# Odd layer's entry: the norm of x ahead of the norm of ctx, both key tiles from one pass over x, values of x between, two query projections in other banks

## The chip, the cores and the metric

The kernel runs on one core of one Trainium2 chip. The metric is the time of one execution on the device in microseconds (us). The time before is the median of three runs, 1648.93 us (1645.26 to 1651.0). TensorE is called PE below, VectorE DVE, ScalarE ACT, GpSimd POOL; SP is the engine whose queue issues nearly all transfers.

## The reference

A block of two layers on a sequence of 512 tokens (x) and 256 context tokens (ctx) of width 1024. The change lies where layer 0 ends (its feed-forward part, for x and ctx) and layer 1, the odd one, begins:

```python
def rmsnorm(x, g):
    xf = x.astype(jnp.float32)
    y = xf * lax.rsqrt(jnp.mean(xf * xf, axis=-1, keepdims=True) + EPS)
    return (y * g.astype(jnp.float32)).astype(x.dtype)

def modulate(x, g, shift, scale):
    return rmsnorm(x, g) * (1 + scale) + shift

def odd_mixer(h, hc, w_qkv, w_out, sink, cos, sin, need_ctx):
    q, k, v = jnp.split(h @ w_qkv, [C_Q_WIDTH, C_Q_WIDTH + C_KV_WIDTH], axis=-1)
    q = apply_rope(q.reshape(b, s_len, C_HEADS, HEAD_DIM), cos, sin)
    k = apply_rope(k.reshape(b, s_len, C_KV_HEADS, HEAD_DIM), cos, sin)
    kc, vc = jnp.split(hc @ w_qkv[:, C_Q_WIDTH:], 2, axis=-1)
```

So x and ctx, both modulated, give keys and values (4 key/value heads of 64, that is two key tiles of 128 rows and one value block of 256 columns); x alone gives queries (16 heads, eight query tiles of 128 rows). Each block of 128 queries attends to a window of up to three blocks of x and to all of ctx, with a sink in the softmax. Output projection, residual and the second feed-forward part follow.

## The kernel before, in words

Activations lie transposed in SBUF: width along the 128 partitions in 8 tiles (k or m, 0 to 7), tokens along the free axis (512 of x, 256 of ctx). All is fp32; a product is made of three matmuls at fp32r (`mm3`, L95, the lines L99, L100, L101): high part by high part, high by low, low by high. So each operand exists as a high part (a cast or copy, by ACT) and a low part (the difference, by DVE or POOL).

Weights come through a ring (`open_ring`, L54; `unit`, L67): SP issues a transfer of 512 columns into a `raw` buffer, ACT casts it to the high part (L75), POOL subtracts for the low part (L78), both into a `w` slot. In `odd` the ring has three raw buffers and four slots (`self.open_ring(512, 3, 4)`). A slot or raw buffer is taken again when its last reader is done; a pool opened in the room of one that closed waits for the last readers of what lay there.

PSUM has three pools of accumulators: `bank` (L45, three buffers, named pb), `fill` (L48, one buffer, pf), and `wide` (L51, two buffers of two banks, pw). Buffers of a pool are given out in turn, in the order in which the program asks for them.

A scheduler puts the instructions of each engine into one fixed list; each engine works through its list in order and stands still at an instruction whose inputs or buffers are not ready. `issue_after(ins)` holds what stands in its block until behind that instruction in the lists.

The stretch that the change touches, in the order of the program:

1. End of the first feed-forward part (L1070 to L1120): for x and then for ctx, the last eight products, each followed by the residual (L757, DVE) and the square (`square`, L769, ACT). The squares of the eight tiles are partly added up (L773, DVE or POOL; tiles 0 to 3) and partly left apart (the list `rest`; tiles 4 to 7).
2. `modulated` for x, then for ctx. Each begins with `rstd_rows` (L135): PE sums squares down the partitions with matmuls against ones (L149 for the sum, L153 for the rest), DVE reads one column per block of 128 tokens (L156) and makes the reciprocal root with integer and Newton steps (L128 to L132; 4 columns for x, 2 for ctx), writes diagonal blocks (L165), and PE spreads them with another product against ones (`spread`, L175). The eight tiles are then modulated (`modulate`, L188): L191 on DVE gives t, L192 on ACT the high part ax, L193 on DVE the low part.
3. `odd`: transfers of the rope tables, the mask and the sink. Then `project_k(0)` and `project_k(1)`: weights of the key tile, all eight k for x, all eight for ctx into one wide buffer, then rope (`rope`, L240: L243 and L244 on DVE, L245 and L246 on POOL), and `stack_k` (L262): casts by ACT (L268, L269) and differences by DVE (L271) that put high and low parts on either half of the partitions.
4. Values: three banks hold six blocks of 128 tokens (four of x, two of ctx), two to a bank; for each k all six blocks. Copies to SBUF at L1168.
5. For each of four groups g: two query tiles (`project_q`, eight products of 512 columns each into `fill`, so one buffer for all eight; then rope and `stack_q`, L253 to L259), then `attend(g, 0)`. An `attend` has for two blocks of queries: four score products (`softmax`, L1200 to L1208, in a wide buffer), their maximum (L1211, DVE), the exponential (L1214, ACT), transposes (L1237, PE) into banks, copies out of them (L1240), and products with the values (L1248, PE) into a bank. After the four groups come four `attend(g, 1)`, then the output projection. The scheduler mixes query products into the attention before them or after them.

Of the kernel before, what the change touches and what calls it, by code (L numbers as in the profile page):

```python
# [6 lines left out]
F32 = mybir.dt.float32  # L7
F32R = mybir.dt.float32r
# [6 lines left out]
P = 128  # L15
D = 1024
KT = D // P
TX = 512
TC = 256
TA = TX + TC  # L20
# [6 lines left out]
class Builder:  # L27
# [39 lines left out]
    def unit(self, src, cols, t=None):  # L67

        nc = self.nc
        w, rb, _ = self.ring_cfg  # L70
        raw = self.ring.tile([P, w], F32, name=self.uid("raw"), tag="raw", bufs=rb)[:, :cols]
        self.last_w = nc.sync.dma_start(raw, src)
        t = t or self.slot()
        hi, lo = t[:, 0, :cols], t[:, 1, :cols]
        nc.scalar.copy(hi, raw)  # L75
        self.nu += 1
        eng = nc.vector if self.dve_lo and self.nu % self.dve_lo == 0 else nc.gpsimd
        eng.tensor_tensor(lo, raw, hi.bitcast(F32), ALU.subtract)  # L78
        return hi, lo

    def blocks(self, src, cols=1024, step=P, t=None):

        w = min(self.ring_cfg[0], cols)
        out = []
        for c in range(0, cols, w):
            n = min(w, cols - c)
            hi, lo = self.unit(src[:, c:c + n], n, t)
            out += [(hi[:, i:i + step], lo[:, i:i + step]) for i in range(0, n, step)]
        return out

# [41 lines left out]
            ve.scalar_tensor_tensor(y, t, 1.5, y, ALU.add, ALU.mult)  # L132
        return y

    def rstd_rows(self, acc, T, inv, bank=None, dg=None, more=(), out=None):  # L135
        return self.spread(self.rstd_diag([(acc, T)], inv, bank, None, dg, more)[0], out or bank)

    def rstd_diag(self, accs, inv, bank=None, eps=None, at=None, more=()):

        nc = self.nc  # L140
        nb = sum(T for _, T in accs) // P
        ms = self.small(nb)
        o = 0
        for acc, T in accs:
            ps = (bank or self.bank)()
            n = T // P
            for j in range(n):
                c = slice(j * P, (j + 1) * P)
                nc.tensor.matmul(ps[:, c], acc[:, c], self.ones, start=j == 0, stop=not more, skip_group_check=True)  # L149
            for t in more:  # L150
                for j in range(n):
                    c = slice(j * P, (j + 1) * P)
                    nc.tensor.matmul(ps[:, c], t[:, c], self.ones, start=False, stop=t is more[-1], skip_group_check=True)  # L153
            col = ps[:, 0:T].rearrange("p (j f) -> p j f", f=P)[:, :, 0]
            if eps is None:
                nc.vector.tensor_scalar(ms[:, o:o + n], col, inv, EPS, ALU.mult, ALU.add)  # L156
# [5 lines left out]
        for acc, T in accs:  # L162
            dg = at if at is not None else self.tmp()
            for j in range(T // P):
                self.last_diag = nc.vector.tensor_scalar(dg[:, j * P:(j + 1) * P], self.ident, r[:, o + j:o + j + 1], None,  # L165
                                                         ALU.mult)
            dgs.append(dg[:, :T])
            o += T // P
        return dgs

    def spread(self, dg, bank=None):

        T = dg.shape[-1]
        out = (bank or self.bank)()
        self.nc.tensor.matmul(out[:, :T], self.ones, dg, start=True, stop=True)  # L175
        return out[:, :T]

    def squares(self, hs, T):
# [593 lines left out]
        elif m:  # L772
            (eng or self.nc.vector).tensor_tensor(sq[:, off:off + n], sq[:, off:off + n], t, ALU.add)  # L773

    def modulated(self, l, sq, off, n, more):

        r = self.rstd_rows(sq[:, off:off + n], n, 1.0 / D, self.bank if off == TX else self.fill, None, more)
        for k in range(KT):
            for w, c, _ in self.cols(off, n):
                self.modulate(self.h(w, k)[:, c], n, self.modcol(l, 1, k, w), self.modcol(l, 0, k, w), r,  # L780
                              [t[:, off:off + n] for t in self.A[k]])


    def ffn_open(self, l, room=None):
# [55 lines left out]
    def ffn(self, l):  # L840
        tc, nc, a = self.tc, self.nc, self.a
        both = l == 0
        self.close_ring()
        T = self.T
        NH = T // 2
        Tp = tc.alloc_tile_pool(name=f"T{l}", bufs=1, side="left", reuse_waits="tile")
# [27 lines left out]
        q = [(m0[:, :NH], m0[:, NH:], m1[:, :NH], m1[:, NH:]) for m0, m1 in zip(self.M[:4], self.M[4:])]  # L874
# [19 lines left out]
        raws, sums, state, Wd, gates = {}, {}, {}, {}, {}  # L894
# [198 lines left out]
        q0 = (4, 5)[l]  # L1093
        more, sqs = [], []
# [25 lines left out]

    def odd(self):
        tc, nc, a = self.tc, self.nc, self.a
        self.open_ring(512, 3, 4)
        X, C = [[[t[:, c] for t in A] for A in self.A] for c in (slice(0, TX), slice(TX, TA))]
        self.hcp.release()
        Rk = tc.alloc_tile_pool(name="kv1", bufs=1, side="right", reuse_waits="tile")
        Rt = tc.alloc_tile_pool(name="rope1", bufs=1, side="right", reuse_waits="tile")
        self.ropep = Rk
        tabs = [self.load(Rk, a[n], [P, TX], n) for n in ("cos", "sin")]
        mraw = self.load(Rt, a["mask"], [P, 384], "mraw")  # L1130
# [9 lines left out]
        K = []  # L1140

        def project_k(n):
            W = self.blocks(a["k1"][n])
            kf = Rt.tile([P, TA], F32, name=self.uid("kf"), tag="kf", bufs=1)
            ps = self.wide()
            for off, T, A in ((0, TX, X), (TX, TC, C)):
                self.dense(ps[:, off:off + T], W, A)
            self.rope(ps[:, :TX], kf[:, :TX], tabs)
            nc.scalar.copy(kf[:, TX:], ps[:, TX:TA])
            K.extend(self.stack_k(kf, Rk, TA, "k1", 8))  # L1150

        for n in range(2):
            project_k(n)

        V = []
        bk = [self.bank() for _ in range(3)]
        acc = [b[:, h * TC:(h + 1) * TC] for b in bk for h in range(2)]
        for kq in range(2):
            W = self.blocks(a["v1"][kq], step=256)
            for i in range(4):  # L1160
                k = kq * 4 + i
                for tb in range(6):
                    A = [X[k][p][:, tb * P:(tb + 1) * P] if tb < 4 else C[k][p][:, (tb - 4) * P:(tb - 3) * P]
                         for p in range(2)]
                    self.mm3(acc[tb], A, W[i], k == 0 and tb % 2 == 0, k == KT - 1)
        for tb in range(6):
            v = Rk.tile([P, TC], F32, name=f"v1_{tb}")
            (nc.vector.tensor_copy if tb % 2 else nc.scalar.copy)(v, acc[tb])  # L1168
            V.append(v)
# [93 lines left out]
        raw = {}  # L1263
# [16 lines left out]
        sq = self.sumsq()  # L1280
# [114 lines left out]
```

## Time and profile before

| what | us |
| --- | --- |
| median of three runs | 1648.93 |
| profiled execution | 1649.09 |
| its span in the trace | 1647.3 |
| mean granted clock of PE | 0.976 |
| PE busy in the span | 1541.4 |
| last ctx product of layer 0 begins | 966.22 |
| spread of x's norm begins | 970.14 |
| first key product begins | 972.84 |
| query tile 0 begins | 1013.55 |
| query tile 1 begins | 1021.79 |
| query tile 5 begins | 1056.07 |

The table's starts are on the trace's own clock, from the start of the span. In the lines of a time view the first number is the start, the second the time from the first start to the last end of the instructions grouped in the row (x4 is four of them); then engine, line of the kernel, operation, output and input by the program's names, and shapes; in brackets the idle time of the engine just before and the instruction that ended it. In a table by stretches the columns are the stretch, its length, busy time and count of PE, PE's weight load, DVE, ACT and POOL, then the granted clock of PE as a share of full speed, the busy share of the DMA engines, and GB/s. With PE alone only its column is there.

### The profile page before, as it was taken

Reading aid. Unit: us, or ns where it says so; the run is one execution under the profiler, and the core shown is the slowest. Engines: PE = TensorE matmul, PEld = TensorE weight load, DVE = VectorE, ACT = ScalarE, POOL = GpSimd, SP = SyncE. Lnnn points to the kernel's source line nnn. Section 1 sums busy time; section 2 is a strip of 40 time slices with the busy share of each in tenths; the row PEclk is TensorE's granted clock in tenths of the full one; section 3 lists DMA queues with packets and bytes.
Section 4 is the critical chain, followed back from the end, with each engine's and each line's share of the span. In section 5 each row is a group of like instructions: output and inputs, shape, how many; then the busy total and the mean of one; then the engine's idle time right before and its main releaser. Section 6 shows DMA issues by size and latency. Waiting matters only on the chain.

```text
span 1647.3 us, 24642 instructions
## 1 busy us (share of the span) xinstructions
PE 1541.4 (94%) x9547; PEld 1366.6 (83%) x9547; DVE 1081.8 (66%) x1991; ACT 719.9 (44%) x1460; POOL 766.9 (47%) x543
## 2 busy tenths in 40 slices
PE   6999989989989999999999999999988999999996
PEld 4776878889988889989989878777868989898886
DVE  4622788866766787666666485666667857666665
ACT  2423675634543233333333244556664544444443
POOL 0463121051166667666666415531313466675662
PEclk9999989989999899999999989999999999999998
DMA  8844100122122333443432012100224132323201
GB/s 316 298 171 149 39 7 1 65 82 112 63 103 94 112 122 125 138 153 115 137 132 90 27 50 79 63 28 19 77 104 141 56 111 90 103 90 103 90 27 52
DMA packets 47957, 161.98 MB, mean 98 GB/s; under 512 B 5472, under 2 KB 9952, under 8 KB 40160
## 3 DMA queue, kind: packets, MB, share of 16 engines
q1 hardware_dynamic: 47696, 160.28, 28.5%
q8 instruction: 75, 1.23, 0.3%
q14 instruction: 42, 0.34, 0.1%
q10 hardware_dynamic: 144, 0.13, 0.1%
HBM read 158.29 MB, written 2.10 MB: 97 GB/s over the span
## 4 chain that ended last, share of the span: by engine, by line
PE 67%; DVE 14%; POOL 5%; DMA 5%; ACT 4%; issue 4%; POOLq 0%; SPq 0%; DVEq 0%; ACTq 0%
PE pw L99 8%; PE pw L100 8%; PE pw L101 8%; PE pb L99 7%; PE pb L100 7%; PE pb L101 7%; POOL w L908 4%; DMA raw<-ffn_in 3%; PE pf L99 2%; PE pf L100 2%; PE pb L1248 2%; PE pf L101 2%; PE pb L1237 2%; DMA rawo<-ffn_out 2%; DVE t L959 2%
## 5 line engine op out<-in xcount | busy, mean ns | idle before, releaser
L99 PE MATMUL pw<-ax,w 128*128 128x384 f32 (+2 forms) x732 | 237.2, 328 | 16.2 <-DVE q L1003 6.6
L78 POOL TENSOR_TENSOR w<-raw,w 128x512 fp32r<-128x512 f32 (+1 forms) x84 | 127.8, 1529 | 248.6 <-ACT w L75 219.5
L100 PE MATMUL pw<-ax,w 128*128 128x384 f32 (+2 forms) x732 | 238.0, 326 | 2.7 <-DVE ax L456 1.3
L101 PE MATMUL pw<-ax,w 128*128 128x384 f32 (+2 forms) x732 | 236.1, 324 | 2.1 <-POOL w L908 2.1
L908 POOL TENSOR_TENSOR w<-raw,w 128x512 fp32r<-128x512 f32 x119 | 179.1, 1519 | 53.0 <-ACT w L904 53.0
L908 POOL TENSOR_TENSOR w<-t,w 128x512 fp32r<-128x512 f32 x90 | 133.6, 1484 | 135.3 <-ACT w L904 131.9
L99 PE MATMUL pb<-hh,w 128*128 128x512 f32 x480 | 167.8, 362 | 13.4 <-ACT hh L115 7.4
L100 PE MATMUL pb<-hh,w 128*128 128x512 f32 x480 | 171.7, 359 | 1.0 <-POOL hh L116 1.0
L101 PE MATMUL pb<-hh,w 128*128 128x512 f32 x480 | 171.2, 358 | 0.0
L757 DVE SCALAR_TENSOR_TENSOR xT<-pb,mod,xT 128x512 f32<-128x512 f32 (+3 forms) x208 | 144.2, 703 | 39.4 <-PE pb L101 38.7
L99 PEld LDWEIGHTS pw<-ax,w 128*128 128x128 f32 x732 | 141.5, 194 | 27.6 <-DVE q L1003 8.2
L99 PE MATMUL pw<-T,w 128*128 128x384 f32 (+1 forms) x508 | 158.7, 313 | 4.9 <-DVE hs L999 2.5
L100 PE MATMUL pw<-T,w 128*128 128x384 f32 (+1 forms) x508 | 158.1, 311 | 4.0 <-DVE T L116 4.0
L101 PE MATMUL pw<-T,w 128*128 128x384 f32 (+1 forms) x508 | 157.6, 310 | 0.0
L100 PEld LDWEIGHTS pw<-ax,w 128*128 128x128 f32 x732 | 142.2, 194 | 11.0 <-DVE ax L456 3.1
L101 PEld LDWEIGHTS pw<-ax,w 128*128 128x128 f32 x732 | 141.7, 194 | 6.1 <-POOL w L908 2.7
L904 ACT CAST w<-t 128x512 fp32r<-128x512 f32 x104 | 64.5, 621 | 179.5 <-DVE t L959 124.6
L908 POOL TENSOR_TENSOR w<-rawo,w 128x512 fp32r<-128x512 f32 x63 | 93.8, 1488 | 68.0 <-ACT w L904 68.0
L99 PEld LDWEIGHTS pb<-hh,w 128*128 128x128 f32 x480 | 89.9, 190 | 26.9 <-ACT hh L115 9.5
L99 PEld LDWEIGHTS pw<-T,w 128*128 128x128 f32 x508 | 96.7, 190 | 10.0 <-DVE hs L999 3.9
L100 PEld LDWEIGHTS pw<-T,w 128*128 128x128 f32 x508 | 96.8, 191 | 6.6 <-DVE T L116 4.6
L101 PEld LDWEIGHTS pb<-hh,w 128*128 128x128 f32 x480 | 90.6, 189 | 13.3
(361 smaller groups left out, 4058.7 us busy)
## 6 DMA issues: line engine op xcount, KB each, us to landing
raw<-ffn_in SPq DMA_DIRECT2D x44, 1024.0 KB, 4.9
ar<-ada SPq DMA_DIRECT2D x24, 1024.0 KB, 7.2
ar<-ada SPq DMA_DIRECT2D x48, 512.0 KB, 3.5
rawo<-ffn_out SPq DMA_DIRECT2D x44, 512.0 KB, 3.9
raw<-odd_out SPq DMA_DIRECT2D x32, 256.0 KB, 2.7
raw<-qk SPq DMA_DIRECT2D x16, 256.0 KB, 8.0
raw<-uv SPq DMA_DIRECT2D x16, 256.0 KB, 2.7
raw<-even_out SPq DMA_DIRECT2D x8, 512.0 KB, 3.5
```

Of the source, the lines that this page charges most:

```text
L78: eng.tensor_tensor(lo, raw, hi.bitcast(F32), ALU.subtract)
L99: mm(out, s[0], m[0], start=start, stop=False, **kw)
L100: mm(out, s[0], m[1], start=False, stop=False, **kw)
L101: return mm(out, s[1], m[0], start=False, stop=stop, **kw)
L757: self.nc.vector.scalar_tensor_tensor(h, ps[:, r], self.modcol(l, j, m, who), h, ALU.mult, ALU.add)
L904: nc.scalar.copy(t[:, 0, :], src)
L908: eng.tensor_tensor(t[:, 1, :], src, t[:, 0, :].bitcast(F32), ALU.subtract)
L959: nc.vector.tensor_tensor(t, x, y, how)
L1237: last = nc.tensor.transpose(pt[:, x * P:(x + 1) * P], es[2 * (x % 2) + x // 2][:, kb * P:(kb + 1) * P], self.ident)
L1248: nc.tensor.matmul(po[64 * h:64 * h + 64, :], V[vb][:, 64 * g:64 * g + 64], t[:, h * TC:h * TC + TC], start=kb == 0, stop=kb == nb - 1, sk ...
```

## The change

- `rstd_diag` is split into `column_sums` (the matmuls against ones) and `rstd_fin` (reciprocal root and diagonal blocks); with `two`, every other diagonal block is written by ACT instead of DVE. `spread` remembers its instruction.
- At the end of layer 0, x's `rstd_rows` stands right behind x's squares and ahead of ctx's products; ctx's column sums are issued behind x's spread. Two tiles are taken from the pool of temporaries and not used, which shifts the turn of its buffers.
- The ring of `odd` has four raw buffers. The weights of both key tiles are loaded first. x is modulated behind their last cast; ctx's reciprocal root comes behind the fifth modulated tile of x.
- Each tile of x is multiplied for both key tiles (two wide buffers) before the next one. Behind the last of these come ctx's spread and its modulation. Tables and mask are issued behind the last key weights.
- The weights of V get four buffers of their own (`own`). The order is: V of x, then the keys of ctx with the stacking of both key tiles, then V of ctx. `kf` has two buffers.
- Query tiles 1 and 3 use `bank` instead of `fill`.

In the order of the built program, ACT's second cast of the key weights waits for ctx's column sums, and x's first modulated tile stands behind that cast. Casts of V's weights stand between x's tiles 1 and 4. Query tile 3, whose bank is taken in turn, stands behind the 102 instructions of the first `attend`.

```diff
-    def rstd_diag(self, accs, inv, bank=None, eps=None, at=None, more=()):
+    def rstd_diag(self, accs, inv, bank=None, eps=None, at=None, more=(), two=False):
+        return self.rstd_fin([(self.column_sums(acc, T, bank, more), T) for acc, T in accs], inv, eps, at, two)
+
+    def column_sums(self, acc, T, bank=None, more=()):
+        ps = (bank or self.bank)()
+        for t in (acc, *more):
+            for j in range(T // P):
+                c = slice(j * P, (j + 1) * P)
+                nc.tensor.matmul(ps[:, c], t[:, c], self.ones, start=t is acc and j == 0,
+                                 stop=t is (more[-1] if more else acc), skip_group_check=True)
+        return ps
...
             for j in range(T // P):
+                if two and j % 2:
+                    nc.scalar.mul(dg[:, j * P:(j + 1) * P], self.ident, r[:, o + j:o + j + 1])
+                    continue
                 self.last_diag = nc.vector.tensor_scalar(dg[:, j * P:(j + 1) * P], self.ident, r[:, o + j:o + j + 1], None,
...
         if both:
             self.A = [self.ax() for _ in range(KT)]
+
+            for _ in range(2):
+                Tp.tile([P, 2 * NH], F32, name=self.uid("sqs"), tag="T", bufs=12)
...
+            if both:
+                if off:
+                    with tc.issue_after(self.last_spread.ins):
+                        self.rows.append(self.column_sums(sq[:, off:off + n], n, self.bank, rest))
+                else:
+                    self.rows.append(self.rstd_rows(sq[:, :n], n, 1.0 / D, self.fill, None, rest, two=True))
             more.append(rest)
-        if both:
-            for q, (off, n) in zip(more, parts):
-                self.modulated(1, sq, off, n, q)
-        else:
+        if not both:
...
     def odd(self):
-        self.open_ring(512, 3, 4)
+        self.open_ring(512, 4, 4)
         X, C = [[[t[:, c] for t in A] for A in self.A] for c in (slice(0, TX), slice(TX, TA))]
+        Wk = [self.blocks(a["k1"][n]) for n in range(2)]
+        self.mods = []
+        with tc.issue_after(self.last_cast.ins):
+            self.modulated(1, 0, TX, self.rows[0])
+        with tc.issue_after(self.mods[4].ins):
+            dg = self.rstd_fin([(self.rows[1], TC)], 1.0 / D)[0]
+
+        pk = [self.wide() for _ in range(2)]
+        for k in range(KT):
+            for n in range(2):
+                last = self.mm3(pk[n][:, :TX], Wk[n][k], X[k], k == 0, k == KT - 1)
+        with tc.issue_after(last.ins):
+            r = self.spread(dg)
+        self.modulated(1, TX, TC, r)
...
+        def own():
+            return Rt.tile([P, 2, 512], F32R, name=self.uid("wv"), tag="wv", bufs=4)
+
+        K, V = [], [None] * 6
+        kfs = []
         for n in range(2):
-            project_k(n)
+            kf = Rt.tile([P, TA], F32, name=self.uid("kf"), tag="kf", bufs=2)
+            self.rope(pk[n][:, :TX], kf[:, :TX], tabs)
+            kfs.append(kf)
+        Wv = sum([self.blocks(a["v1"][kq], step=256, t=own) for kq in range(2)], [])
+        acc = [b[:, h * TC:(h + 1) * TC] for b in [self.bank() for _ in range(3)] for h in range(2)]
+
+        def project_v(tbs):
+            for k in range(KT):
+                for tb in tbs:
+                    A = [X[k][p][:, tb * P:(tb + 1) * P] if tb < 4 else C[k][p][:, (tb - 4) * P:(tb - 3) * P]
+                         for p in range(2)]
+                    with tc.issue_after(last.ins) if k == tb == 0 else ExitStack():
+                        self.mm3(acc[tb], A, Wv[k], k == 0 and tb % 2 == 0, k == KT - 1)
+            for tb in tbs:
+                V[tb] = Rk.tile([P, TC], F32, name=f"v1_{tb}")
+                (nc.vector.tensor_copy if tb % 2 else nc.scalar.copy)(V[tb], acc[tb])
+
+        project_v(range(4))
+        for n in range(2):
+            self.dense(pk[n][:, TX:TA], Wk[n], C)
+            nc.scalar.copy(kfs[n][:, TX:], pk[n][:, TX:TA])
+            K.extend(self.stack_k(kfs[n], Rk, TA, "k1", 8))
+        project_v((4, 5))
...
         def project_q(n):
-            ps = self.fill()
+            ps = (self.bank if n in (1, 3) else self.fill)()
```

More of the change, by code (lines that the diff above doesn't have):

```diff
@@ L133, in rsqrt_small, with rstd_rows, rstd_fin @@
         return y
-    def rstd_rows(self, acc, T, inv, bank=None, dg=None, more=(), out=None):
-        return self.spread(self.rstd_diag([(acc, T)], inv, bank, None, dg, more)[0], out or bank)
-    def rstd_diag(self, accs, inv, bank=None, eps=None, at=None, more=()):
-        nc = self.nc
-        nb = sum(T for _, T in accs) // P
-        ms = self.small(nb)
+    def rstd_rows(self, acc, T, inv, bank=None, dg=None, more=(), out=None, two=False):
+        return self.spread(self.rstd_diag([(acc, T)], inv, bank, None, dg, more, two)[0], out or bank)
+    def rstd_diag(self, accs, inv, bank=None, eps=None, at=None, more=(), two=False):
+        return self.rstd_fin([(self.column_sums(acc, T, bank, more), T) for acc, T in accs], inv, eps, at, two)
+    def column_sums(self, acc, T, bank=None, more=()):
+        nc = self.nc
+        ps = (bank or self.bank)()
[5 more added lines that the diff above has]
+        return ps
+    def rstd_fin(self, sums, inv, eps=None, at=None, two=False):
+        nc = self.nc
+        ms = self.small(sum(T for _, T in sums) // P)
+        nb = ms.shape[-1]
         o = 0
-        for acc, T in accs:
-            ps = (bank or self.bank)()
+        for ps, T in sums:
             n = T // P
[L147 to L153, printed above, removed]
             col = ps[:, 0:T].rearrange("p (j f) -> p j f", f=P)[:, :, 0]
@@ L174, in spread @@
         out = (bank or self.bank)()
-        self.nc.tensor.matmul(out[:, :T], self.ones, dg, start=True, stop=True)
+        self.last_spread = self.nc.tensor.matmul(out[:, :T], self.ones, dg, start=True, stop=True)
         return out[:, :T]
@@ L773, in square, with modulated @@
             (eng or self.nc.vector).tensor_tensor(sq[:, off:off + n], sq[:, off:off + n], t, ALU.add)
-    def modulated(self, l, sq, off, n, more):
-        r = self.rstd_rows(sq[:, off:off + n], n, 1.0 / D, self.bank if off == TX else self.fill, None, more)
+    def modulated(self, l, off, n, r):
         for k in range(KT):
             for w, c, _ in self.cols(off, n):
-                self.modulate(self.h(w, k)[:, c], n, self.modcol(l, 1, k, w), self.modcol(l, 0, k, w), r,
-                              [t[:, off:off + n] for t in self.A[k]])
+                self.mods.append(self.modulate(self.h(w, k)[:, c], n, self.modcol(l, 1, k, w), self.modcol(l, 0, k, w), r,
+                                               [t[:, off:off + n] for t in self.A[k]]))
     def ffn_open(self, l, room=None):
@@ L1128, in odd @@
         self.ropep = Rk
-        tabs = [self.load(Rk, a[n], [P, TX], n) for n in ("cos", "sin")]
-        mraw = self.load(Rt, a["mask"], [P, 384], "mraw")
+        with tc.issue_after(self.last_w.ins):
+            tabs = [self.load(Rk, a[n], [P, TX], n) for n in ("cos", "sin")]
+            mraw = self.load(Rt, a["mask"], [P, 384], "mraw")
         mask = Rk.tile([P, 384], F32R, name="mask")
@@ L1138, in odd @@
         nc.vector.tensor_scalar(nsink, nsink, -1.0, None, ALU.mult)
[L1140 to L1150, printed above, removed]
```

20 lines of the change are left out of this document (4 added, 16 removed).

## The prediction

> **What bounds the kernel now.** I read the page first (busy shares, the chain that ended last), then tables of busy time by stage, then the rows of each engine in time order around the odd layer's entry, and last TensorE alone in steps of 3.413 us, because the granted clock in the records changes on such steps.
>
> ```profile
> PE 1541.4 (94%) x9547; PEld 1366.6 (83%) x9547; DVE 1081.8 (66%) x1991; ACT 719.9 (44%) x1460; POOL 766.9 (47%) x543
> ...
> PE 67%; DVE 14%; POOL 5%; DMA 5%; ACT 4%; issue 4%; POOLq 0%; SPq 0%; DVEq 0%; ACTq 0%
> ```
>
> TensorE (PE) is busy 94% of the span and holds 67% of the last chain. So an edit of order can win only what PE spends idle or at half clock, and it loses what it adds of these. The stages (columns: length, then busy time and count of PE, weight load, DVE, ACT, POOL, then granted clock, DMA share, GB/s):
>
> ```profile
> 958.30:972.84 14.54, 11.54 (x94) 10.54 (x92) 11.05 (x37) 5.27 (x13) 1.99 (x2) 0.97 0.29 87
> 972.84:1013.55 40.71, 39.40 (x242) 35.15 (x243) 27.67 (x51) 18.58 (x32) 17.91 (x13) 0.89 0.23 72
> 1013.55:1056.00 42.45, 36.70 (x175) 29.86 (x174) 27.03 (x45) 20.65 (x38) 27.27 (x21) 0.96 0.22 69
> 1056.00:1100.00 44.00, 44.00 (x279) 32.79 (x277) 26.77 (x62) 25.49 (x58) 19.72 (x18) 1.00 0.14 43
> ```
>
> Norms up to the first key matmul (972.84), keys and values up to query tile 0 (1013.55), query tiles 0 to 4 with the first softmaxes (to 1056), attention. From 1056 on PE has no hole: nothing is to be won there. The holes before it:
>
> ```profile
> 966.79 1.95 PE L153 MATMUL pb<-ones,sqs 128*128 128x128 f32 x16
> 970.14 1.10 PE L175 MATMUL pf<-q,ones 128*128 128x512 f32 x2 [1.40 <-DVE sm L156]
> 972.84 0.80 PE L99 MATMUL pw<-ax,w 128*128 128x512 f32 x1 [1.59 <-ACT ax L192]
> ...
> 1021.79 0.47 PE L99 MATMUL pf<-ax,w 128*128 128x512 f32 x1 [2.61 <-DVE qf L244]
> 1030.85 0.50 PE L99 MATMUL pf<-ax,w 128*128 128x512 f32 x1 [1.13 <-DVE qf L244]
> 1039.13 0.50 PE L99 MATMUL pf<-ax,w 128*128 128x512 f32 x1 [1.15 <-DVE qf L244]
> 1047.57 0.50 PE L99 MATMUL pf<-ax,w 128*128 128x512 f32 x1 [0.86 <-DVE qf L244]
> ```
>
> The last four rows are the first matmuls of query tiles 1 to 4: each waited for the rope of the tile before it (L244), which empties the one bank that all query tiles share. And the clock (PE alone):
>
> ```profile
> 968.47:971.88 3.41, 1.37 (x5) 1.00 0.27 77
> 971.88:975.29 3.41, 2.42 (x5) 0.50 0.00 0
> 975.29:978.71 3.42, 2.86 (x8) 0.50 0.49 153
> 978.71:982.12 3.41, 3.41 (x10) 0.50 0.25 77
> 982.12:985.53 3.41, 3.41 (x17) 1.00 0.02 5
> ...
> 1019.67:1023.08 3.41, 1.29 (x6) 1.00 0.18 46
> 1023.08:1026.49 3.41, 3.41 (x10) 0.50 0.36 108
> ```
>
> A step in which PE works 1.29 or 1.37 of 3.41 us is followed by half clock, and full clock comes back only behind a full step (3.41), not behind 2.42 or 2.86. Half clock costs half of the busy time spent in it. How the matmuls of 512 columns follow each other, 0.43 at half and 0.23 at full clock:
>
> ```profile
> 978.60 0.63 PE L99 MATMUL pw<-ax,w 128*128 128x512 f32 x1
> 979.03 0.63 PE L100 MATMUL pw<-ax,w 128*128 128x512 f32 x1
> ...
> 983.20 0.40 PE L101 MATMUL pw<-ax,w 128*128 128x512 f32 x1
> 983.43 0.39 PE L100 MATMUL pw<-ax,w 128*128 128x512 f32 x1
> ```
>
> **What can be won.** In 1013.55 to 1056: idle 42.45 - 36.70 = 5.75, and 3.41 / 2 = 1.7 of half clock: 7.45 us. In the entry: what PE's busy time misses in the steps from 968.47 on, 2.04 + 0.99 + 0.56 = 3.6 (the idle times in the rows, 1.40 and 1.59, lie in it), and (2.42 + 2.86 + 3.41) / 2 = 4.3 of half clock: 7.9, of which some must stay, since a norm's chain lies there.
>
> **Part 1: x's norm ahead of ctx's.** Before, x's column sums (32 pieces; the last 16 at 962.77) are split by ctx products, of 256 columns at 0.12 each:
>
> ```profile
> 961.83 0.28 PE L99 MATMUL pb<-hh,raw 128*128 128x256 f32 x1
> 961.95 0.28 PE L100 MATMUL pb<-hh,raw 128*128 128x256 f32 x1
> ...
> 962.77 1.95 PE L153 MATMUL pf<-ones,sqs 128*128 128x128 f32 x16
> ```
>
> ```profile
> 963.37 0.94 DVE L773 TENSOR_TENSOR sq<-sq,sqs 128x256 f32<-128x256 f32 x2
> 964.75 0.16 DVE L156 TENSOR_SCALAR sm<-pf 128x4 f32<-128x4 f32 x1 [0.44 <-PE pf L153]
> ...
> 965.11 0.48 DVE L757 SCALAR_TENSOR_TENSOR ctxT<-pb,mod,ctxT 128x256 f32<-128x256 f32 x1
> ...
> 968.12 1.88 DVE L165 TENSOR_SCALAR q<-ident,sm 128x128 f32<-128x128 f32 x4
> ```
>
> After, they run in one piece, and DVE reads them (L156's step) about 1.1 us sooner, at 963.65. But in the order of the built program DVE now does within the reciprocal root six ctx residual adds (before three behind that read, at 965.11, 965.83 and 966.54) and two sums of squares (before ahead of it): 3 x 0.40 + 2 x 0.47 = 2.1 more. Against this: 1.1 from the earlier start, and the diagonal blocks split between DVE and ACT, 1.88 / 2 = 0.94 saved. Sum +0.1, so the spread stays at about 970.1: **x's norm does not come earlier.** PE meanwhile runs out: in before the ctx column sums (4 + 16 pieces up to 968.74) filled it; these are now held until behind the spread. PE is idle from about 966.5 (the last ctx product, its matmuls being the same) to 970.1. So the step 965.06 to 968.47 holds 1.4 us of work instead of 3.41, and by the rows above half clock begins at 968.47, one step sooner. The spread then takes about 1.8 instead of 0.9 (two rows, 1.10 with their overlap), the column sums start at 971.9 and need 2.2 at full, 4.4 at half clock: 3.4 fill the step to 975.29, whose full busy time brings full clock back, and the rest ends at 975.8.
>
> **Part 2: a wait on ACT that is new.** The second key tile's weights are cast into slots that lie on the squares of ctx, so the second of the four casts waits for those column sums; ACT works in order, and behind it stand two casts and x's first modulated tile, for which PE waits.
>
> ```profile
> 967.39 0.60 ACT L75 CAST w<-raw 128x512 fp32r<-128x512 f32 x1
> 972.06 0.72 ACT L192 ACTIVATE ax<-t,mod 128x512 fp32r<-128x512 f32 x1 [4.07 <-DVE t L191]
> 972.69 1.12 ACT L75 CAST w<-raw 128x512 fp32r<-128x512 f32 x2
> ```
>
> ```profile
> 973.37 2.62 POOL L78 TENSOR_TENSOR w<-raw,w 128x512 fp32r<-128x512 f32 x2 [4.04 <-ACT w L75]
> ```
>
> Three casts of 0.56: 975.9 + 1.7 = 977.6, the tile (0.72) to 978.3, the first key matmul at 978.4, 5.6 later than before. The step to 978.71 is nearly empty, so 978.71 to 982.12 is at half clock once more: 8 of the 48 x key matmuls at 0.43 then 0.227. Behind tiles 0 and 1 stand on ACT casts of V's weights, which wait for raw buffers freed by POOL's low parts (three left at 1.3 each from 976.5: 977.9, 979.2, 980.4) and a transfer:
>
> ```profile
> raw<-odd_out SPq DMA_DIRECT2D x32, 256.0 KB, 2.7
> raw<-qk SPq DMA_DIRECT2D x16, 256.0 KB, 8.0
> ```
>
> At 2.7 us (the same size of tile with short queues, and DMA shares here are 0.00 to 0.49; at 8.0 tile 2 would come some 5 later and x's keys end some 4 later), casts at 980.6, 981.9, 983.1, tiles 2 to 4 at 981.9, 983.2, 984.4 and so on at 1.4 apart; six matmuls per tile, 1.4 together, just keep up with them, the last tile at about 988.5, its low part and matmuls: x's keys end near 991. Then ctx's spread (0.3), V of x (96 matmuls of 256 columns at 0.119, 11.4), ctx's keys (48: 5.7), V of ctx (48: 5.7), and 0.4 of hand-overs, 23.5 together, with modulated ctx tiles, wv's parts and both ropes beside it on engines that stand at 27.67 of 40.71 (DVE) and less. Query tile 0 starts at 1014.5, not 1013.55: **+1.0**. At full clock from the sums on they end at 973.2, the first tile follows at 975.7 and x's keys end at 988.4: -1.6.
>
> The Trainium skill, "TensorE: Matmul & The Clock Gate", Part 1, speaks for the second: it lets the clock fall after an idle window of about 3.4 us, free-running. No such step here is wholly idle (the gap from 966.5 to 970.1 leaves work in both steps that it touches), so by it the sum would hold -1.6 in place of +1.0. This trace differs: half clock came behind 1.29 and 1.37 us of work, and the rows decide.
>
> **Part 3: query tiles.** Tiles 0, 1, 2 now have banks of their own and run on, and both key tiles' stacking moves from in front of tile 0's rope to beside V of ctx:
>
> ```profile
> 1016.20 4.06 DVE L271 TENSOR_TENSOR kl<-kf,kh 64x768 fp32r<-64x768 f32 x4 [1.61 <-ACT kh L268]
> ...
> 1020.19 0.73 DVE L243 STREAM_SHUFFLE sh<-pf 128x512 f32<-128x512 f32 x1
> ```
>
> In before, tile 0's rope starts behind this L271 group: that made the 2.61 stall and the half clock behind it. After, the second key tile's four of these end about a query tile ahead of it. What stays is tile 4's wait for tile 2's rope, with only two short score groups between, 0.45. **-7.0** of the 7.45. If its cover fails (stacking still late), 2.6 + 1.7 come back.
>
> **Part 4: attention loses filler.** Tile 3's bank is taken in turn behind the first attention unit's. So the unit's 102 instructions behind tile 4, before mixed with tiles 3 to 5, stand alone; exponentials, PSUM copies and products hand over to each other there, each wait in order.
>
> ```profile
> 1100.00:1150.00 50.00, 49.48 (x369) 37.62 (x368) 31.83 (x75) 29.97 (x76) 9.32 (x11) 1.00 0.04 11
> ```
>
> This row is attention with few or no query matmuls left: 0.52 idle in 50. The unit's 17 us or so would then lose 0.2 to 0.9; the first has no unit ahead of it to lean on. From the other side, an exposed hand-over at each of eight softmaxes costs one exponential of about 0.7 and its maximum: some 6 in all (an estimate). I take **+0.8**, near the rows, and keep 0 to 6. The weights, casts and SP issues of tiles 3 to 7 move with them and have slack (POOL 19.72 of 44). Below nothing is possible too: tiles 3, 5, 6, 7 now fill later holes; I bound it by 1, twice the row's 0.52.
>
> **Sum**: +1.0 - 7.0 + 0.8 = -5.2. Profiled execution: span 1647.3 of 1649.09 us; 1649.09 is 0.16 above the median 1648.93 of three, so I subtract from 1649.09 and get 1643.9.
>
> **The rivals.**
> - *Entry at full clock*, worked out in Part 2: 1649.09 - 1.6 - 7.0 + 0.8 = 1641.3, with Part 4 at -1 and all 7.45 won 1639.0. For it: the 1.4 of work in the step is from a walk by rows, and how much work holds the clock is not in them. Against: the 1.37 row. It is the case of the rule that Part 2 quotes from the Trainium skill.
> - *Gain given back in attention*: Part 4 at +4 to +6, 1647 to 1649; for it, in-order waits with no neighbour, against it the 49.48 of 50.
> - *Slower: attention in a clock trap.* If the first unit pays the whole 6 of exposed hand-overs, spread over its five steps of 3.41, each step holds about 2.2 of work; once one falls to the 1.3 of the rows the clock halves, and it stays there, since no step is full any more: up to 6 of the unit's 17 us of work at half clock would cost 6 more. +12, 1649.09 + 1.0 - 7.0 + 12 = 1655.1. It decides from 6.0 lost in the unit on, by over 0.3% from 10.9 on. For it: a step of 2.86 at half clock did not end it. Against: the row of attention.
> - *The bank does not come free*: the stalls of the query tiles stay (tile 1 waits for V's copies or stacking), 1649.09 + 1.0 - 3 = 1647.
>
> **How the numbers follow.** 0.3% (4.9 us) is about what a measurement can tell from no change. Forecast (1642.3 to 1646) 0.35; entry at full clock 0.23; given back 0.17; bank not free 0.09; slower 0.16. The forecast lies at the bound (1644.0): 0.22 of it I count as faster, 0.13 as the same. Faster 0.22 + 0.23 = 0.45; same 0.13 + 0.17 + 0.09 = 0.39; slower by over 0.3%: 0.16. The range must take in full clock with all won (1639) and reach toward the slower case, most of which it leaves out: 1638 to 1654.
>
> **What would show it.** Right: the first spread at 970 to 970.3; ACT idle ahead of the second key cast until PE's ctx sums; half clock from 968.47's counterpart on; first key matmul about 978; query tile 0 near 1014.5, tiles 1 and 2 with no wait; PE idle of 1 to 2 in the first attention unit. Wrong: a spread before 969.5; a waiting query tile 1; half clock inside attention; a first key matmul after 981.

## The result, and the profile after

The changed kernel takes 1664.88 us (median of five, 1660.51 to 1666.31) against 1645.26 before (five, 1641.85 to 1651.0): ratio 1.0102, 95% interval 1.0083 to 1.0122. By the ratio that is some 17 us slower (14 to 20); the medians differ by 19.6. The forecast was 5 us faster; 1664.88 lies outside its range.

Where the time went is read with three marks that both traces have: x's first column sum, the first matmul of query tile 0, and the spread in the norm of the first half behind the attention. TensorE alone, before (columns: stretch, length, busy time and count, granted clock, DMA share, GB/s):

```profile
959.02:1013.55 54.53, 50.22 (x330) 0.91 0.24 77
1013.55:1201.09 187.54, 179.66 (x1206) 0.99 0.16 49
1201.09:1647.30 446.21, 410.94 (x2835) 0.97 0.26 89
```

and after:

```profile
960.91:1015.00 54.09, 47.94 (x330) 0.97 0.20 61
1015.00:1215.31 200.31, 183.25 (x1206) 0.98 0.14 45
1215.31:1663.80 448.49, 412.00 (x2835) 0.97 0.25 88
```

The entry is 0.4 shorter, the query tiles and attention are 12.8 longer, the rest 2.3; 1.9 more lie ahead of the first mark. (That mark itself scatters from 953.4 to 961.6 among all profiled executions of this study, whose work up to there is nearly the same.) In the middle stretch PE is idle 17.1 us instead of 7.9, and busy 3.6 longer with the same count of matmuls; two steps at half clock instead of one account for about 1.7 of that. A unit below is one `attend`. All rows of PE with a wait, from tile 0 to 1111, in the changed kernel:

```profile
1033.52 0.39 PE L1228 MATMUL pw<-kh,qa 128*128 128x256 f32 x1 [1.42 <-DVE qa L267]
...
1043.85 0.44 PE L1228 MATMUL pw<-kh,qa 128*128 128x384 f32 x1 [2.97 <-ACT e L1242]
...
1047.43 0.44 PE L1265 MATMUL pb<-ident,e 128*128 128x128 f32 x2 [1.48 <-ACT e L1242]
...
1055.57 0.44 PE L1265 MATMUL pb<-ident,e 128*128 128x128 f32 x2 [0.23 <-ACT e L1242]
1056.57 0.65 PE L1276 MATMUL pb<-pt,v 128*64 128x256 f32 x4 [0.57 <-ACT pt L1268]
...
1070.12 0.50 PE L99 MATMUL pf<-ax,w 128*128 128x512 f32 x1 [2.40 <-DVE qf L252]
...
1076.33 0.39 PE L1228 MATMUL pw<-kh,qa 128*128 128x256 f32 x1 [0.47 <-DVE qa L267]
...
1079.11 0.50 PE L99 MATMUL pf<-ax,w 128*128 128x512 f32 x1 [1.12 <-DVE qf L252]
...
1086.41 0.50 PE L99 MATMUL pf<-ax,w 128*128 128x512 f32 x1 [0.55 <-DVE qf L252]
...
1096.90 0.58 PE L99 MATMUL pf<-ax,w 128*128 128x256 f32 x1 [1.55 <-DVE qf L252]
...
1105.61 0.44 PE L1265 MATMUL pb<-ident,e 128*128 128x128 f32 x2 [1.60 <-ACT e L1242]
```

Tiles 1 and 2 do start without a wait: no row of theirs is here. Tile 3 runs from 1061.79 to 1067.3, right behind the first attention unit (before, it started at 1039.13, inside it). The first row is the first scores waiting for the stacking of tile 1. The next four, 5.3 us together, are the first unit waiting for its own exponentials and PSUM copies. The other six, 7.7 us, come behind tile 3: tiles 5 to 7, the second unit, and the product that takes the fill bank next. DVE shows that tile 4, whose products were done by 1040.0, had its rope only behind tile 3's (the lines with pf), so the fill bank stood shut for 30 us:

```profile
1067.54 0.72 DVE L251 STREAM_SHUFFLE sh<-pb 128x512 f32<-128x512 f32 x1
1068.17 0.67 DVE L252 TENSOR_TENSOR qf<-pb,cos 128x512 f32<-128x512 f32 x1
...
1068.77 0.73 DVE L251 STREAM_SHUFFLE sh<-pf 128x512 f32<-128x512 f32 x1
1069.39 0.68 DVE L252 TENSOR_TENSOR qf<-pf,cos 128x512 f32<-128x512 f32 x1
```

The entry, PE and ACT of the changed kernel:

```profile
970.97 1.13 PE L183 MATMUL pf<-q,ones 128*128 128x512 f32 x2 [2.33 <-ACT q L171]
971.93 0.61 PE L148 MATMUL pb<-ones,sq 128*128 128x128 f32 x4
972.38 1.95 PE L148 MATMUL pb<-ones,sqs 128*128 128x128 f32 x16
976.30 0.73 PE L99 MATMUL pw<-ax,w 128*128 128x512 f32 x2 [1.97 <-ACT ax L200]
```

```profile
970.83 0.60 ACT L75 CAST w<-raw 128x512 fp32r<-128x512 f32 x1
973.96 1.66 ACT L75 CAST w<-raw 128x512 fp32r<-128x512 f32 x3 [2.54 <-issue]
975.53 1.33 ACT L200 ACTIVATE ax<-t,mod 128x512 fp32r<-128x512 f32 x2
```

x's norm is spread 10.06 us behind the first column sum (11.12 before), but the first key matmul comes 15.39 behind it (13.82 before): ACT stands still for 2.54, then makes three casts, then x's first tile. The profile names no releaser for that wait; that it is for ctx's sums is shown by e7 below, where the sums come earlier and ACT makes all four casts without it.

### The profile page after: what moved, and what is told of

The parts are those of the page before. It is cut to its first block, busy times and chain, and to the rows that moved or that the text cites. A ratio compares the mean times of both kernels' runs of the same rounds, so it can differ in the third digit from the quotient of the medians.

```text
span 1663.8 us, 24639 instructions
## 1 busy us (share of the span) xinstructions
PE 1545.5 (93%) x9547; PEld 1368.5 (82%) x9547; DVE 1088.6 (65%) x1989; ACT 721.5 (43%) x1462; POOL 772.0 (46%) x543
## 5 line engine op out<-in xcount | busy, mean ns | idle before, releaser
L78 POOL TENSOR_TENSOR w<-raw,w 128x512 fp32r<-128x512 f32 (+1 forms) x80 | 120.1, 1509 | 223.6 <-ACT w L75 201.1
L99 PEld LDWEIGHTS pb<-hh,w 128*128 128x128 f32 x480 | 89.8, 190 | 27.8 <-ACT hh L115 10.1
L99 PE MATMUL pb<-ax,w 128*128 128x256 f32 (+2 forms) x336 | 103.9, 311 | 2.4 <-ACT w L911 2.4
L99 PEld LDWEIGHTS pw<-T,w 128*128 128x128 f32 x508 | 97.1, 191 | 10.3 <-DVE hs L1006 3.8
L101 PE MATMUL pb<-ax,w 128*128 128x256 f32 (+2 forms) x336 | 103.3, 309 | 2.1 <-DVE w L78 2.1
```

Of the source, the lines that this page charges most:

```text
L99: mm(out, s[0], m[0], start=start, stop=False, **kw)
L101: return mm(out, s[1], m[0], start=False, stop=stop, **kw)
```

## The experiments

Theory A: the loss is made by query tile 3's place behind the first attention unit. Theory B: by the new entry. The table gives the ratio to the kernel before with its 95% interval, and from each profiled execution the two stretches between the marks above (first sum to tile 0, tile 0 to the spread). Each ratio is to runs of the kernel before taken together with that kernel's, so the ratios compare better than the medians.

| kernel | median us | ratio (95%) | entry | tiles and attention |
| --- | --- | --- | --- | --- |
| before | 1645.26 | | 54.5 | 187.5 |
| changed | 1664.88 | 1.0102 (1.0083 to 1.0122) | 54.1 | 200.3 |
| e1 all tiles in fill | 1647.07 | 1.0006 (0.9986 to 1.0026) | 55.7 | 187.4 |
| e2 only tile 1 in a bank | 1645.13 | 1.0004 (0.9987 to 1.0022) | 54.1 | 187.7 |
| e3 banks alone, old entry | 1660.29 | 1.0090 (1.0064 to 1.0116) | 53.6 | 202.6 |
| e4 tile 1's bank alone | 1649.98 | 1.0016 (0.9996 to 1.0037) | 53.5 | 191.7 |
| e5 tile 3 early | 1652.64 | 1.0045 (1.0028 to 1.0063) | 54.1 | 190.9 |
| e6 tile 5 late | 1659.63 | 1.0087 (1.0061 to 1.0113) | 54.2 | 198.9 |
| e7 e2, sums free | 1646.77 | 1.0009 (0.9994 to 1.0024) | 51.4 | 189.3 |
| e8 e5, sums free | 1647.46 | 1.0013 (0.9995 to 1.0030) | 51.4 | 190.9 |
| e9 own rope buffers | 1658.25 | 1.0091 (1.0066 to 1.0115) | 54.1 | 202.1 |
| e10 tile 5, own buffers | 1666.92 | 1.0131 (1.0110 to 1.0153) | 55.7 | 202.2 |
| e11 e1, sums free | 1644.70 | 0.9989 (0.9971 to 1.0008) | 51.4 | 186.8 |
| e12 another unit between | 1651.92 | 1.0032 (1.0016 to 1.0048) | 55.8 | 206.8, one unit more |
| e13 its control | 1651.90 | 1.0027 (1.0010 to 1.0045) | 54.8 | 204.2, one unit more |
| e14 tile 7 late | 1660.66 | 1.0084 (1.0060 to 1.0107) | 54.1 | 200.0 |

**Which part of the change costs.** Four kernels: the changed one without the other banks, with one of them, and the kernel before with both or one.

```diff
-            ps = (self.bank if n in (1, 3) else self.fill)()
+            ps = self.fill()
```

is e1; e2 has `n in (1,)` there. The other two edit the kernel before, e3 as below and e4 with `n in (1,)`:

```diff
-            ps = self.fill()
+            ps = (self.bank if n in (1, 3) else self.fill)()
```

> The changed kernel with all eight query tiles back in the one fill bank (nothing else undone). Theory A (the loss comes from query tile 3 being placed behind the first attention unit, because its bank is taken in turn): the unit is mixed with tiles 3 to 5 again, idle time from query tile 0 to the second half's norm spread falls from 17 to about 7 us, and the time falls by 12 to 17 us to about 1650 or below, near the kernel before. Theory B (the loss comes from the new entry: keys and values ready in another order, so that attention starts before its inputs flow): the time stays within 4 us of the changed kernel, about 1661 to 1665.

> The changed kernel with only query tile 1 in another bank; tile 3 is back in fill. Theory A: tile 3 stands ahead of the first attention unit again, so nearly all of the loss goes, as in the kernel with all tiles in fill, and tile 1 no longer waits: 1640 to 1648. Theory B: 1661 to 1665.

> The kernel before with query tiles 1 and 3 in other banks and nothing else of the change. Theory A: tile 3 again stands behind the first attention unit, so 10 to 16 us are lost with the old entry too: 1655 to 1662. Theory B: as the kernel before or a little faster, 1640 to 1646.

> The kernel before with only query tile 1 in another bank. Theory A: no loss; tile 1 starts without its wait of 2.61 us and the half clock behind it is not entered: 0 to 4 us faster than the kernel before. Theory B: the same as that, so this run measures only what the second bank for tile 1 is worth by itself.

One line in the old kernel (e3) makes the whole loss, and taking it out of the new one (e1, e2) removes it: theory B is out. The middle stretch of e3:

```profile
1007.83:1210.44 202.61, 184.97 (x1207) 0.97 0.14 45
```

e4 was expected 0 to 4 us faster and is not; its middle stretch is 4.2 longer. Ahead of 1100 its waits are 0.98 and 4.28, where before has 2.61, 1.13, 1.15 and 0.86; they sum to 0.5 less, but two steps at half clock follow the long one, where before has one step. And e2, in which tiles 0 to 2 run without a wait and tile 3 is in time, gains nothing over e1. Ten-us slices of e2, from 100 us behind tile 0 on:

```profile
1109.10:1119.10 10.00, 9.27 (x67) 1.00 0.01 2
1119.10:1129.10 10.00, 9.72 (x70) 1.00 0.01 2
```

and the same of the kernel before:

```profile
1113.55:1123.55 10.00, 10.00 (x79) 1.00 0.01 2
1123.55:1133.55 10.00, 10.00 (x75) 1.00 0.01 2
```

Up to 100 us e2 was ahead, by 581 matmuls to 566; at 120 us it is level, 718 to 720. The waits that went at the query tiles came back as thinner attention. Not all of them went: in e2 the first scores still wait 1.42, and tile 4 2.26:

```profile
1037.22 0.50 PE L99 MATMUL pf<-ax,w 128*128 128x512 f32 x1 [2.26 <-DVE qf L252]
```

**The bank, or the place.**

```diff
-        for g in range(4):
-            project_q(2 * g)
-            project_q(2 * g + 1)
-            attend(g, 0)
+        for n in range(4):
+            project_q(n)
+        attend(0, 0)
+        for g in range(1, 4):
+            if g > 1:
+                project_q(2 * g)
+                project_q(2 * g + 1)
+            attend(g, 0)
```

is e5; e6 has `n in (1, 5)` instead of `(1, 3)`.

> The changed kernel, with query tiles 1 and 3 still in other banks, but tiles 2 and 3 asked for ahead of the first attention unit, so that tile 3's bank comes ahead of the unit's banks in the turn. In the built order tile 3 then stands right behind tile 2 and tiles 4 to 7 stand inside the first units. Theory A (the place of tile 3 behind the whole first unit is the cause): the loss goes, 1641 to 1649. Theory C (a query tile in a bank of the attention's own is the cause, wherever it stands, since it takes a third of them): 1655 or more.

> The changed kernel with query tiles 1 and 5 in other banks instead of 1 and 3. Tile 5's bank is then taken in turn behind the second attention unit's, and it stands behind that unit in the built order; tile 3 is mixed into the first unit. Theory A: a loss of the same kind, smaller because the first unit keeps its filler and tiles 6 and 7 stand ahead: 1649 to 1658. Theory A' (it is the start of attention alone that can't do without filler): no loss, 1641 to 1648.

e5: with tile 3 still in a bank but ahead of the unit, more than half of the loss goes (1.0045 against 1.0102); its median misses what A and C expected both. e6: tile 5, late in the same way behind the second unit, costs 14 us (a little above what A expected) though the start of attention kept its filler, so A' falls. The place decides most, not the bank.

**The entry.** e7 is e2, and e8 is e5, with

```diff
-                    with tc.issue_after(self.last_spread.ins):
-                        self.rows.append(self.column_sums(sq[:, off:off + n], n, self.bank, rest))
+                    self.rows.append(self.column_sums(sq[:, off:off + n], n, self.bank, rest))
```

> The changed kernel with only tile 1 in another bank, and ctx's column sums not held behind x's spread; in the built order they stand ahead of it, and the casts of the key weights no longer wait behind the spread. If the held sums cost the entry what my walk says (an idle PE of some 2.3 us ahead of the spread and the casts behind the sums), the stretch from x's first column sum to query tile 0 falls from 54 to 51 to 52 us and the time to 2 to 3 us below the one-bank kernel: 1640 to 1644. If the entry is set by something else (the weights, the tiles' own pace), it stays at 54 and the time at about 1645.

> Tile 3 early and the sums not held, together. Theory A and the walk of the entry: tiles 0 to 3 run without waits, no filler is missed, and the entry gains its 2 to 3 us: 1637 to 1643, faster than the kernel before. Theory C: 1653 or more.

The sums now fill PE ahead of the spread, and the key matmuls follow 2.6 us sooner behind the first sum (12.79 for 15.39):

```profile
968.86 0.71 PE L148 MATMUL pb<-ones,sq 128*128 128x128 f32 x4
969.40 1.95 PE L148 MATMUL pb<-ones,sqs 128*128 128x128 f32 x16
971.30 1.13 PE L183 MATMUL pf<-q,ones 128*128 128x512 f32 x2
974.02 0.73 PE L99 MATMUL pw<-ax,w 128*128 128x512 f32 x2 [1.60 <-ACT ax L200]
```

The entry falls to 51.4 in every such kernel, as expected. In the whole time e7 doesn't show it (1.0009 against e2's 1.0004): the runs of one kernel scatter by 10 us, and 1.6 went again in e7's attention. e8 does: taken together with e5, its median is 5.2 us lower (1.0013 against 1.0045; the means of the twelve runs each differ by 4.6, with a 95% interval of some 2.7 either way). Neither is faster than the kernel before, which was expected of both.

**Why a late tile costs.** First idea (A1): tile 3 keeps tile 4 from its rope, which shuts the fill bank, so the unit lacks query products to fill it. e9 gives the tiles in banks rope buffers of their own (`rope` takes the tag of its buffer); e10 does it to e6:

```diff
-            qf = Rs.tile([P, TX], F32, name=self.uid("qf"), tag="qf", bufs=2)
-            self.rope(ps, qf, tabs)
+            own = n in (1, 3)
+            qf = Rs.tile([P, TX], F32, name=self.uid("qf"), tag="qfb" if own else "qf", bufs=1 if own else 2)
+            self.rope(ps, qf, tabs, "shb" if own else "sh")
```

> The changed kernel, query tiles 1 and 3 still in other banks and tile 3 still asked for and issued behind the first attention unit, but the rope buffers (sh, qf) of tiles 1 and 3 are of their own, so that tile 4's rope no longer takes its turn behind tile 3's. In the built order tile 3 still stands behind the unit, and tiles 5 and 6 now stand inside it. Theory A1 (tile 3 late keeps tile 4 unroped, so the fill bank is shut for the whole unit and no query tile can fill it): most of the loss goes, 1644 to 1653. Theory A2 (tile 3's own lateness, which holds up the second unit, is what costs): the loss stays, 1657 to 1665.

> The same for the kernel with tiles 1 and 5 in other banks: tile 5 stays behind the second unit, tile 7 now stands ahead of tile 5 inside the units. Theory A1: most of the 14 us of that kernel go, 1646 to 1653. Theory A2: 1656 to 1663.

A1 falls: the loss stays, and is larger in e10 (1.0131) than in e6 (1.0087). In e9 the first unit is full (tiles 5 and 6 are in it), and the hole opens behind tile 3 (1064.45 to 1070.15) instead. PE beside the first unit up to within tile 3, from there on, and the wait there:

```profile
1035.70:1067.50 31.80, 31.06 (x175) 0.95 0.16 50
1067.50:1100.00 32.50, 24.11 (x126) 0.84 0.09 33
```

```profile
1069.76 0.39 PE L101 MATMUL pb<-ax,w 128*128 128x512 f32 x1
1070.00 0.38 PE L1266 MATMUL pb<-ident,e 128*128 128x128 f32 x2
1076.14 0.58 PE L1229 MATMUL pw<-kh,qa 128*128 128x256 f32 x1 [5.77 <-DVE qa L267]
```

5.77 us is tile 3's way from its last product through rope and stacking (DVE, POOL, ACT, DVE) to the second unit's scores. The wait also brings three steps of half clock, from 1074.16 on, with 7.0 us of work in them, so some 3.5 us more. In the changed kernel the same way was partly covered by tiles 5 to 7, which then lacked in the first unit: one set of fillers, two gaps.

That gives A2: the second unit needs tile 3, so nothing of it can overlap the first one. e12 puts the second half of group 0, which needs no tile 3, between (and has five output buffers instead of four); e13 is the same on the kernel before; e14 has `n in (1, 7)`.

```diff
             project_q(2 * g + 1)
+            if g == 1:
+                attend(0, 1)
             attend(g, 0)
...
-        for g in range(4):
+        for g in range(1, 4):
             attend(g, 1)
```

> The changed kernel, banks as in the change and tile 3 still behind the first unit, but the second half of group 0 (which needs tiles 0 and 1 alone) is done right behind the first unit instead of later; one more output buffer. Theory A2 (the second unit has to wait for tile 3, and nothing else is there to overlap): the loss against its control e13 falls from 15 to 6 us or less. Theory A3 (a late query tile costs as filler): it stays at 10 us or more.

> The kernel before with that same order of attention units and buffer, and nothing of the change: within 4 us of the kernel before, the base for e12. Both theories say the same here.

> The changed kernel with tiles 1 and 7 in other banks: tile 7 stands behind the third unit, and the fourth needs it. The second halves stand behind it in the program. Theory A2: the fourth unit waits for tile 7 as the second did for tile 3, 8 to 16 us over the kernel before, unless second halves are put in between. Theory A3: smaller, since tiles 3 to 6 all stand ahead as filler, 0 to 8 us.

With other work between, the loss over the control is gone as far as the runs can tell (1.0032 against 1.0027, each with an interval of some 3 us either way; the control is itself 4.4 us over the kernel before, a little more than expected). In the profiles e12's stretch is 2.6 longer than e13's, so a small loss is not ruled out. Tile 3 still stands behind the first unit and tile 4's rope behind tile 3's. All waits of PE in e12 from tile 4 to 1112:

```profile
1039.15 0.44 PE L1228 MATMUL pw<-kh,qa 128*128 128x384 f32 x1 [2.98 <-ACT e L1242]
1043.49 0.69 PE L1265 MATMUL pb<-ident,e 128*128 128x128 f32 x2 [1.07 <-ACT e L1242]
1111.44 0.44 PE L1265 MATMUL pb<-ident,e 128*128 128x128 f32 x2 [1.65 <-ACT e L1242]
```

So the first unit, without filler, still waits 4.1 us, about what the query tiles save (5.0 in e13, 1.4 here). What is gone are the waits behind tile 3, 7.7 us in the changed kernel. And the last tile, late behind the third unit, costs 14 us with all other tiles ahead of it, since the fourth unit needs it:

```profile
1121.91 0.58 PE L1228 MATMUL pw<-kh,qa 128*128 128x256 f32 x1 [4.98 <-DVE qa L267]
```

A2 stands; A3 (late filler, whoever needs it) falls as the whole cause. It keeps a part: in e14 units 2 and 3, left without filler, wait 3.5 us before that. No kernel here beats the kernel before beyond its interval; e11, the new entry with free sums and all tiles in fill, comes nearest (0.9989).

> The new entry with ctx's column sums not held and all query tiles in fill: the stretch from the first column sum to query tile 0 was 51.4 us with free sums against 54.5 before, the stretch from there to the second norm 187.4 with all tiles in fill against 187.5. If stretches add up, 2 to 4 us faster than the kernel before, 1641 to 1645; if the scatter of the clock eats it, within 0.2% of it.

Its stretches add up to 4 us less than before's; the ratio says 1.8 (0.9971 to 1.0008), so this is not settled.

## Why the prediction was wrong, point by point

- **The step that failed is Part 4**: "The unit's 17 us or so would then lose 0.2 to 0.9", taken as +0.8. It saw tile 3 move behind the unit and asked what the unit loses without filler. Measured, the first unit waits 5.3, within the 0 to 6 that the part kept, and 7.7 more follow behind tile 3, for which the part has no term. The row it leaned on, 49.48 of 50, is attention in which each unit overlaps the next (the scores of one, L1200, stand at 1118.85, ahead of the last transposes of the one before it, L1259 at 1119.78). It didn't ask who needs tile 3: the second unit, which by that is cut off from the first. The price is of the pair: e9 fills the first unit and loses as much, e12 leaves it bare and loses nothing that the runs can tell.
- **Part 3, -7.0, was wrong too**. Tiles 0 to 2 ran without waits as said, and the stacking was in time, so what it named as its risk did not happen. But where it kept 0.45 of wait, 1.42 stayed in the changed kernel and 3.9 in e2. And e2, which has just this part and tile 3 in time, is idle 7.5 in the whole stretch against 7.9, and no faster. "From 1056 on PE has no hole: nothing is to be won there" holds for the stretch shown there (44.00 of 44.00), and hid that the query tiles used sooner are missed later. Parts 3 and 4 together were forecast at -6.2 and measured at +12.8.
- **Part 1 and 2, +1.0**: measured -0.4, but this is not settled: the entry scatters from 53.5 to 54.8 in the profiles with the old one (before, e3, e4, e13) and from 54.1 to 55.8 with the new one and held sums. Some of its steps were wrong. The spread came 10.06 behind the first sum; it was walked as 970.1, 11.1 behind 959.02, so x's norm does come 1.1 sooner: from DVE's read to the spread it took 5.39 in both kernels, where the walk added 1.2. That is 969.1 on the clock of before, which the prediction lists as a sign of being wrong. The wait on ACT, three casts, then the tile came as walked (2.54 idle, 1.66 of casts). The first key matmul was walked at 978.4, 19.4 behind the first sum, and measured at 15.39. The half clock expected ahead of it did not come: the step from 967.09 held 1.55 us of work and the next ran at full clock (the walk's own case at full clock has 16.7), and the norm was 1.1 sooner. One step of half clock came behind it instead, from 977.33. Tile 0 came 54.1 behind the first sum, forecast 55.5. The held sums cost 2.7 (e7 against e2), which the walk had as a new wait without pricing its removal.
- **The rivals**: "gain given back in attention" names the right place, at +4 to +6 where the first unit alone waits 5.3 and the waits behind tile 3 add 7.7. The slower one named the trap of half clock inside the first unit; the changed kernel shows none there, and two steps of it later (from 1096.79 and 1107.03, 1.7 us each at most). In e3 and e12 it is there: three steps, from 1036.7 and from 1039.76, behind waits of 5.14 and 2.98. "The bank does not come free" didn't happen.
- **The chances** put 0.16 on slower. The bounds of Part 4, 0 to 6, came from one unit's own hand-overs; the exposed way of a query tile to the next unit's scores was in the traced rows (tile 0's rope, casts and differences between 1020.19 and 1029) and was not added.

Left open: 2.3 us of the slowdown lie behind the attention, in a stretch that scatters from 442.9 to 447.2 in the other profiles with the same order of units; and why e5 keeps 7 us in its runs while its profiled execution shows 3.4 in the middle. That execution is one of the two fastest of e5's twelve (1647.65, median 1652.64), and what sets the fast ones apart is not known.

## What to carry to other kernels

When an edit gives an operation another buffer of a pool that is handed out in turn, look up what now stands ahead of it in the built order, and then who consumes it: a producer moved behind a whole unit cuts the next unit off from that one. Holes of the bounding engine are a gain only if the work that would fill them isn't what fills another place. With a fixed set of fillers, price both places together, and don't take the idle share of a stretch where units overlap for one where they can't.

## What the runs showed of the hardware that was not expected

Near the limit, busy time in a 3.413 us step does not by itself tell what the clock does next. In the changed kernel, and then in e9:

```profile
967.09:970.50 3.41, 1.55 (x13) 1.00 0.00 0
970.50:973.91 3.41, 2.94 (x20) 1.00 0.00 2
973.91:977.33 3.42, 1.15 (x6) 1.00 0.30 91
977.33:980.74 3.41, 2.98 (x7) 0.50 0.66 201
980.74:984.15 3.41, 3.14 (x13) 1.00 0.50 157
...
1103.62:1107.03 3.41, 1.81 (x15) 1.00 0.00 0
1107.03:1110.45 3.42, 3.42 (x17) 0.50 0.00 0
```

```profile
1070.75:1074.16 3.41, 0.00 (x0) 1.00 0.37 129
1074.16:1077.57 3.41, 1.43 (x6) 0.50 0.04 13
```

Steps with 1.15 and 1.81 us of work are followed by half clock, one with 1.55 is not. A half-clock step with 2.98 of work was enough to end it, where before 2.42 and 2.86 were not, and in e12 one with 3.10 (from 1043.17) was not. So no single threshold in busy time, such as the walk used, fits these traces, on either side.

Over all such steps of the sixteen traces of this study there are bands. Every full-clock step with less than 1.5 us of PE work was followed by half clock (165 of them), none with more than 1.95 was, and between the two 42 of 141 were. No half-clock step with less than 2.85 of work ended it, and every one with more than 3.15 did. The walk expected 1.4 us of work in the step ahead of ctx's sums, just below the first band; it held 1.55, just inside.

An entirely idle step (0.00, from 1070.75 in e9) was followed by half clock. The Trainium skill, "TensorE: Matmul & The Clock Gate", Part 1, has half clock after such an idle window, and this trace agrees.
